# Hybrid SSD and GLA trunk: 21 units' y turned by transposing transfers, and the first block's gates reordered

## The chip, the cores and the metric

The kernel runs on one core of a Trainium2 chip. The metric is the device time of one execution in microseconds (us); lower is better. In the views of the profile PE is the matrix engine (PEld its weight loads), DVE the vector engine, ACT the scalar engine, POOL the general engine and SP the engine that issues most transfers. A name with q (ACTq, POOLq) is the engine's sequencer, where register work, waits and DMA issues are.

## What is computed

2048 tokens of width 1024, with 16 meta tokens in front, pass one layer of two parallel branches. Cut to what matters here:

```python
u = rmsnorm(hres, norm_w)
proj = jnp.einsum('bld,dn->bln', u, w_in)
z, xbc, dt_raw, q, k, v, g_gla, a_lr, merge_g = split_cols(proj, IN_WIDTHS)
xbc = jax.nn.silu(causal_depthwise_conv(xbc, conv_w, conv_b))
...
y = y.reshape(b, l, D_SSD) * jax.nn.silu(z)
y_ssd = rmsnorm(y.reshape(b, l, SSD_GROUPS, D_SSD // SSD_GROUPS),
                ssd_norm_w.reshape(SSD_GROUPS, -1)).reshape(b, l, D_SSD)
gate_logit = jnp.einsum('blr,rk->blk', a_lr, gla_gate_w2) + gla_gate_b
log_a = (jax.nn.log_sigmoid(gate_logit.astype(jnp.float32)) / GLA_GATE_TEMP)
...
o = rmsnorm(jnp.concatenate([o_m, o_r], axis=1), gla_norm_w)
y_gla = o.reshape(b, l, GLA_DV) * jax.nn.silu(g_gla)
branches = jnp.stack([y_ssd.astype(y_gla.dtype), y_gla], axis=2)
branch_proj = jnp.einsum('blnc,ncd->blnd', branches, w_branch)
gates = jax.nn.sigmoid(merge_g.reshape(b, l, N_BRANCH, D_MODEL))
merged = jnp.sum(gates * branch_proj, axis=2)
return hres + jnp.einsum('bld,de->ble', merged, w_out)
```

SSD is a scan over chunks of 128 tokens in 4 groups (256 channels each, a 128-wide state), GLA a gated linear attention with 4 heads of 256 value channels.

## The kernel before

**Tiling.** The tokens go in 4 blocks of 512 (`BLK`), the first with the 16 meta tokens in front (`m0` is 16 there and 0 elsewhere). In each block every SSD group and every GLA head is one unit: 4 + 4 units, 32 in all. After the blocks, from some 1500 us on, follow the products for the merge gates, the two branches and the output, which the change leaves alone. All large products are in single precision, made of three matmuls on high and low parts (`accum`, L205 to L209); so L207, L208 and L209 are the projections wherever they stand in a view.

**What sets the order.** PE's and SP's order is written by hand: `enter` (L950) yields one piece of a projection after another, and after each piece `step` advances every running generator by one yield. `begin` adds a generator. So a scan is a chain of short steps, each put on PE behind one piece of a projection. The order of DVE, ACT and POOL is left to a scheduler that sees the instructions' dependences; `tc.issue_after(x)` keeps what stands under it behind instruction x on its engine. Each engine works through its list in order, and each waits at an instruction whose operand isn't there.

**The units' ends.** `ssd_scan` (L588) works through 4 chunks of 128 tokens. `before(c)` turns the features (L634 on PE), makes xdt, xw and the skip part (L637 to L640, DVE), bt (L643, ACT) and the decay matrix dm (four L647 and one L649 on ACT, L650 on DVE). `after(c)` has the products L659, L660 and L662 on PE, the state's decay L664 (POOL) and its sum L665 (DVE), the output L667 to L672 (DVE) and its square sum L674 (ACT). When 4 chunks are done `rstd_of` gives the norm's factor (L251 on DVE, L252 on POOL), L689 scales the tile `yt` (tokens on partitions, 4 x 256 channels, from the pool "tok4" with 5 buffers) and the unit is turned to channels on partitions: 2 x 4 transposes of 128x128 on PE (L694) into two banks of PSUM (pool `pt`, 3 banks), two evictions with the channel weights on ACT (L696) into "gg", two stores to `y_left` that ACT issues (L697). `gla_scan` (L739) ends alike: scale L920 of `ot` (one buffer), transposes L925, then the product with the gate on DVE (L926) straight from PSUM, stores L929.

**The convolution** (`proj_conv`): ACT takes a projection out of PSUM twice (L565 raw, L566 scaled), DVE adds three shifted taps (L570), ACT's tanh (L573) and DVE's L574 end it.

**The GLA gates** (`gates`, L451): matmuls into PSUM, DVE's L473 and ACT's L474 read them, ACT's L476 and L477 make the logarithm for two heads at a time, then DVE subtracts (L480) and sums along the tokens (`tensor_tensor_scan`, L482). Their result `g_all` is read by `gla_scan` alone (from L751 on). In the first block `gates` begins at step 6 and `ssd_scan` of group 0 too. z's gates are L491 (ACT) and L492 (DVE).

**Others named below.** L334 to L336 prepare u of the next block (`fetch_u`; L335 is its store), L83 to L87 sum weights for the later products (`make_sums`, POOL and transfers), L171 and L172 split weights, `atp` holds GLA's attention split into two parts (L256, 2 buffers), L888 and L909 are PE's in GLA, L801 and L835 its levels and states. `behind()` keeps the decay matrices of the first block behind the last eviction of a projection.

Of the kernel before, what the change touches and what calls it, by code (L numbers as in the profile page):

```python
# [9 lines left out]
F32R = mybir.dt.float32r  # L10
BF16 = mybir.dt.bfloat16
U8 = mybir.dt.uint8
AF = mybir.ActivationFunctionType
ALU = mybir.AluOpType

P = 128
# [5 lines left out]
SG = 4  # L22
# [21 lines left out]
def trunk_kernel(ctx: ExitStack, tc: tile.TileContext, xm, xmt, w_feat, w_tok, w_v3, w_zm, w_br, w_o,  # L44
# [7 lines left out]
    def mk(pool, shape, dt, tag, **kw):  # L52
        cnt[0] += 1
        return pool.tile(shape, dt, tag=tag, name=f"{tag}_{cnt[0]}", **kw)
# [194 lines left out]
    def rstd_of(ssq, n, scale):  # L249
        r = mk(sm, [P, 4], F32, "rstd")  # L250
        nc.vector.tensor_scalar(r[:, :n], ssq, scale, EPS, op0=ALU.mult, op1=ALU.add)  # L251
        nc.gpsimd.tensor_tensor(r[:, :n], r[:, :n], mhalf[:, :n], op=ALU.pow)  # L252
        return r
# [197 lines left out]
    def gates(o):  # L451
        m0, tt, chunks, g_all = o.m0, o.tt, o.chunks, o.g_all
        ast = (mk(wk, [P, META + BLK], F32R, "act", bufs=NACT) if m0 else mk(wk, [P, BLK], F32R, "sq", bufs=NSQ))[:48, :tt]
        for a, n in ([(0, META), (m0, BLK)] if m0 else [(0, BLK)]):
            ps = bank(pt, "pt")
            for i, (ca, cn) in enumerate(chunks):
                if a <= ca < a + n:
                    nc.tensor.transpose(ps[:48, ca - a:ca - a + cn], o.alr[:cn, i], ident[:cn, :cn])
            nc.scalar.activation(ast[:, a:a + n], ps[:48, :n], AF.Copy)
            nc.vector.tensor_tensor(ast[:32, a:a + n], ps[:32, :n], ast[:32, a:a + n].bitcast(F32),  # L460
                                    op=ALU.subtract)
            nc.scalar.activation(ast[:16, a:a + n], ps[:16, :n], AF.Copy)
        yield
        for h2 in range(0, GH, 2):
            gmt = mk(wk, [P, 2, META + BLK], F32, "tok4", bufs=NT4)
            for h in (h2, h2 + 1):
                gm = gmt[:, h % 2, :tt]
                gb = gate_b[:, h:h + 1]
                for i, (a, n) in enumerate(o.segs_all):
                    ps = bank(*((pj, "pj") if m0 and i == 0 else (pt, "pt")))  # L470
                    nc.tensor.matmul(ps[:, :n], w2[:, h * P:(h + 1) * P], ast[:, a:a + n],
                                     start=True, stop=True)
                    nc.vector.tensor_scalar(gm[:, a:a + n], ps[:, :n], gb, 0.0, op0=ALU.add, op1=ALU.min)  # L473
                    nc.scalar.activation(g_all[:, h, a:a + n], ps[:, :n], AF.Abs, bias=gb)  # L474
            ga = g_all[:, h2:h2 + 2, :tt]
            nc.scalar.activation(ga, ga, AF.Exp, scale=-1.0)  # L476
            nc.scalar.activation(ga, ga, AF.Ln, bias=1.0)  # L477
            yield
            for h in (h2, h2 + 1):
                nc.vector.tensor_tensor(gmt[:, h % 2, :tt], gmt[:, h % 2, :tt], g_all[:, h, :tt], op=ALU.subtract)  # L480
                for a, n in chunks:
                    nc.vector.tensor_tensor_scan(g_all[:, h, a:a + n], ones[:, :n], gmt[:, h % 2, a:a + n], 0.0,  # L482
                                                 op0=ALU.mult, op1=ALU.add)
                yield


# [68 lines left out]
    def proj_conv(o, g):  # L555
        tt = o.tt
        feats = o.feats[g] = []
        for j in range(4):
            ti = g * 4 + j
            pss = proj_feat(f"s{ti}", w_feat[T_SSD + ti], o.segs_all, o.mov)  # L560
            cin = mk(spool, [P, 3 + META + BLK], F32, "cin")
            acc = mk(spool, [P, META + BLK], F32, "acc")[:, :tt]
            nc.scalar.activation(cin[:, 0:3], tails[:, ti, :], AF.Copy)
            for ps, (a, n) in zip(pss, o.segs_all):
                nc.scalar.activation(cin[:, 3 + a:3 + a + n], ps[:, :n], AF.Copy)  # L565
                evicted[:] = [nc.scalar.activation(acc[:, a:a + n], ps[:, :n], AF.Identity, scale=hcw[:, ti, 3:4],  # L566
                                                   bias=hcb[:, ti:ti + 1])]
            nc.gpsimd.tensor_copy(tails[:, ti, :], cin[:, tt:tt + 3])
            for k in range(3):
                nc.vector.scalar_tensor_tensor(acc, cin[:, k:k + tt], hcw[:, ti, k:k + 1], acc,  # L570
                                               op0=ALU.mult, op1=ALU.add)
            f = mk(wk, [P, META + BLK], F32, "act", bufs=NACT)
            nc.scalar.activation(f[:, :tt], acc, AF.Tanh)  # L573
            nc.vector.scalar_tensor_tensor(f[:, :tt], f[:, :tt], 1.0, acc, op0=ALU.add, op1=ALU.mult)  # L574
            feats.append(f)
            yield

    cbs, evicted = {}, []

    def behind():  # L580
        return tc.issue_after(evicted[-1].ins) if evicted else nullcontext()
# [2 lines left out]
    def fetch_cb(o, g, c):  # L584
        cbs[g, c] = cb = mk(spool, [P, 4, P], F32, "cb", bufs=3)
        nc.sync.dma_start(cb, o.cumd[4 * g:4 * g + 4, c * P:(c + 1) * P].unsqueeze(0).to_broadcast([P, 4, P]))

    def ssd_scan(o, g):  # L588
        m0, ci0 = o.m0, o.ci0
# [63 lines left out]
        def after(c):  # L653
            a = m0 + c * P
            ci = ci0 + c
            xdt, xw, bt, dm = held.pop(c)
            py = bank(pc, "pc")
            for h in range(4):
                nc.tensor.matmul(py[:, h * 64:(h + 1) * 64], dm[:, h], xdt[:, h], start=True, stop=True)  # L659
            nc.tensor.matmul(py[:, 256:512], cf[:, a:a + P], s_ssd[:, g], start=True, stop=True)  # L660
            pst = bank(pc, "pc")
            nc.tensor.matmul(pst[:, :256], bt, xw.rearrange("p a c -> p (a c)"), start=True, stop=True)  # L662
            sv = s_ssd[:, g].rearrange("p (h c) -> p h c", c=64)
            nc.gpsimd.tensor_tensor(sv, sv, hb(dec[:, ci, hs], P), op=ALU.mult)  # L664
            nc.vector.tensor_tensor(s_ssd[:, g], s_ssd[:, g], pst[:, :256], op=ALU.add)  # L665
            yo = mk(wk, [P, 4, 64], F32, "c1", bufs=NC1)
            nc.vector.tensor_tensor(yo, py[:, 256:512].rearrange("p (h c) -> p h c", c=64),  # L667
                                    hb(ecu[:, ci, hs], P), op=ALU.mult)
            yof = yo.rearrange("p a c -> p (a c)")
            nc.vector.tensor_tensor(yof, yof, py[:, 0:256], op=ALU.add)  # L670
            nc.vector.tensor_tensor(yof, yof, yt[:, c], op=ALU.add)
            nc.vector.tensor_tensor(yt[:, c], yof, o.zs[g][:, c], op=ALU.mult)  # L672
            jk = mk(wk, [P, 256], BF16, "junk", bufs=1)
            nc.scalar.activation(jk, yt[:, c], AF.Square, accum_out=ssq[:, c:c + 1])  # L674

        before(0)
        yield
# [2 lines left out]
            yield  # L680
        for c in range(1, NCH):
            before(c)
            after(c - 1)
            yield
        after(NCH - 1)
        yield
        r = rstd_of(ssq, 4, 1.0 / 1024)
        for c in range(NCH):
            nc.scalar.activation(yt[:, c], yt[:, c], AF.Identity, scale=r[:, c:c + 1])  # L689
        yield  # L690
        for j in range(2):
            ps = bank(pt, "pt")
# [46 lines left out]
    def gla_scan(o, h, last=False):  # L739
# [178 lines left out]
        r = rstd_of(ssq, 4, 1.0 / 256)  # L918
        for c in range(NCH):
            nc.scalar.activation(ot[:, c], ot[:, c], AF.Identity, scale=r[:, c:c + 1])  # L920
        yield
        for j in range(2):
            ps = bank(pt, "pt")
            for c in range(NCH):
                nc.tensor.transpose(ps[:, c * P:(c + 1) * P], ot[:, c, j * P:(j + 1) * P], ident)  # L925
            nc.vector.scalar_tensor_tensor(gs[j], ps, hgw[:, j:j + 1], gs[j], op0=ALU.mult, op1=ALU.mult)  # L926
# [7 lines left out]
    def begin(gen):  # L934
        begun.append(gen)
# [14 lines left out]
    def enter(pieces, o):  # L950
        b = o.b
        for n in range(6 * (SG + GH) + 1):
            i, r = divmod(n, 6)
            if r == 0:
                if 0 < i <= SG:
                    begin(ssd_scan(o, i - 1))
                elif i > SG and not (b == nblk - 1 and i - SG > LATE_G):
                    begin(gla_scan(o, i - SG - 1))
                if (b, i) in beside:
                    begin(beside_unit(beside[b, i]))  # L960
            if n == (8 if b else 6):
                begin(gates(o))
            if n == 6 * SG + (3 if b else 3):
                begin(fetch_u(b + 1) if b + 1 < nblk else first_b())
            if n < 6 * (SG + GH):
                yield next(pieces)
        assert next(pieces, pieces) is pieces
# [496 lines left out]
```

## Time and profile before

| | |
|---|---|
| median of 3 runs | 2273.96 us (2271.23 to 2276.47) |
| profiled execution | 2273.81 us, of which the span of the profile is 2271.3 |
| busiest engines | PE 2222.4, DVE 1565.7, ACT 1185.6, POOL 679.9 us |
| mean granted PE clock | 0.994 |

A row of the view by lines tells what a group of like instructions cost; a timeline row is start, duration, engine, line, instruction, and in brackets how long the engine had idled before it and what ended that. Matmuls overlap: PE's duration of one (0.39 us for 128x512) is longer than the step to the next (0.23 us).

### The profile page before, as it was taken

The page shows a single profiled execution, that of the slowest core. Times are in us where ns is not written, and L with a number is a line of the kernel's source. Part 1 is how long each engine was busy: PE and PEld are TensorE (multiplying, and loading weights), DVE is VectorE, ACT ScalarE, POOL GpSimd, SP SyncE. Part 2 cuts the span into 40 slices and gives each one's busy share as a digit, 9 for nine tenths or more (in the row PEclk, how much of TensorE's full clock was granted, in tenths as well). Part 3 has the DMA queues.
Part 4 walks back from the last instruction along what each step waited for, and adds up shares of the span by engine and source line. Part 5 has one row for each costly group of instructions (what it writes and reads, how often), then busy time and mean ns, then how long its engine had stood idle before and what let it go on. Part 6 is the DMA issues. An engine that isn't in the chain of part 4 may idle for free.

```text
span 2271.3 us, 34896 instructions
## 1 busy us (share of the span) xinstructions
PE 2222.4 (98%) x11789; PEld 1902.9 (84%) x11789; DVE 1565.7 (69%) x2935; ACT 1185.6 (52%) x2767; POOL 679.9 (30%) x681
## 2 busy tenths in 40 slices
PE   7999999999999999999999999999999999999998
PEld 6899989888888988888988888878888888888887
DVE  5777666677667676557677566674678955779876
ACT  4666655456544455544456454454554545554544
POOL 3334443122221112122122200056323264413341
PEclk9999999999999999999999999999999999999999
DMA  8666776667778667788676664366677866678763
GB/s 298 219 215 233 256 243 223 219 213 235 242 246 269 210 208 228 230 256 280 202 225 215 214 212 161 117 221 223 220 250 258 306 230 205 240 270 268 242 194 126
DMA packets 314210, 517.94 MB, mean 228 GB/s; under 512 B 28080, under 2 KB 162480, under 8 KB 314032
## 3 DMA queue, kind: packets, MB, share of 16 engines
q1 hardware_dynamic: 246864, 419.63, 57.4%
q10 hardware_dynamic: 67168, 96.10, 11.7%
q8 instruction: 92, 1.51, 0.3%
q14 instruction: 86, 0.70, 0.1%
HBM read 368.42 MB, written 147.19 MB: 227 GB/s over the span
## 4 chain that ended last, share of the span: by engine, by line
PE 87%; DVE 4%; ACT 3%; DMA 3%; issue 2%; POOL 1%; SPq 0%; POOLq 0%; ACTq 0%; DVEq 0%
PE pj L207 19%; PE pj L209 19%; PE pj L208 19%; PE pt L207 4%; PE pt L208 4%; PE pt L209 4%; PE pc L209 2%; PE pc L208 2%; PE pc L659 2%; PE pc L207 2%; PE pc L801 2%; PE pc L660 1%; PE pc L909 1%; PE pc L662 1%; PE pt L634 1%
## 5 line engine op out<-in xcount | busy, mean ns | idle before, releaser
L207 PE MATMUL pj<-ue,whl 128*128 128x264 f32 (+1 forms) x672 | 236.9, 353 | 8.4 <-ACT acc L566 4.1
L209 PE MATMUL pj<-ue,whl 128*128 128x264 f32 (+1 forms) x672 | 231.1, 344 | 0.8 <-DVE tkc L419 0.8
L208 PE MATMUL pj<-ue,whl 128*128 128x264 f32 (+1 forms) x672 | 230.2, 343 | 0.0
L207 PE MATMUL pj<-uo,whl 128*128 128x512 f32 x512 | 206.0, 402 | 0.0
L209 PE MATMUL pj<-uo,whl 128*128 128x512 f32 x512 | 200.1, 391 | 0.0
L208 PE MATMUL pj<-uo,whl 128*128 128x512 f32 x512 | 199.4, 389 | 0.0
L207 PE MATMUL pj<-b,a 128*128 128x512 f32 (+1 forms) x484 | 188.9, 391 | 1.5 <-ACT sn L1109 1.0
L209 PE MATMUL pj<-b,a 128*128 128x512 f32 (+1 forms) x484 | 188.8, 390 | 0.0
L208 PE MATMUL pj<-b,a 128*128 128x512 f32 (+1 forms) x484 | 188.0, 388 | 0.6 <-DVE b L1050 0.5
L570 DVE SCALAR_TENSOR_TENSOR acc<-cin,hcw,acc 128x512 f32<-128x512 f32 (+1 forms) x192 | 153.1, 798 | 50.2 <-ACT acc L566 49.2
L83 POOL TENSOR_TENSOR wr<-wr 128x256 f32<-128x256 f32 x80 | 66.8, 835 | 384.5 <-DMA wr<-y 162.6
L1065 POOL TENSOR_TENSOR as<-ar,ar 128x512 f32<-128x512 f32 x40 | 57.9, 1447 | 386.0 <-DMA ar<-in_w_br 103.2
L1075 DVE TENSOR_TENSOR a<-ar,a 128x512 fp32r<-128x512 f32 x160 | 129.3, 816 | 58.9 <-ACT a L1074 54.6
L1050 DVE TENSOR_TENSOR b<-br,b 128x512 fp32r<-128x512 f32 x140 | 124.7, 910 | 43.7 <-ACT b L1049 43.1
L207 PEld LDWEIGHTS pj<-ue,whl 128*128 128x128 f32 x672 | 127.7, 190 | 24.7 <-ACT acc L566 5.1
L209 PEld LDWEIGHTS pj<-ue,whl 128*128 128x128 f32 x672 | 127.8, 190 | 15.9 <-POOL whl L172 1.0
L208 PEld LDWEIGHTS pj<-ue,whl 128*128 128x128 f32 x672 | 127.8, 190 | 14.7
L1049 ACT ACTIVATE b<-br 128x512 fp32r<-128x512 f32 x140 | 86.5, 627 | 100.6 <-DMA br<-br_t 38.8
L172 POOL TENSOR_TENSOR whl<-wr,whl 128x512 fp32r<-128x512 f32 (+1 forms) x76 | 99.0, 1310 | 126.4 <-ACT whl L171 84.8
L1075 DVE TENSOR_TENSOR a<-as,a 128x512 fp32r<-128x512 f32 x120 | 105.5, 881 | 39.0 <-ACT a L1074 35.7
L1109 ACT ACTIVATE sn<-pj 128x512 f32<-128x512 f32 x118 | 69.8, 591 | 110.8 <-PE pj L209 69.5
L208 PE MATMUL pt<-b,a 128*128 128x512 f32 x320 | 125.3, 391 | 0.0
(329 smaller groups left out, 6470.7 us busy)
## 6 DMA issues: line engine op xcount, KB each, us to landing
whl<-k_s SPq DMA_DIRECT2D x96, 512.0 KB, 3.7
whl<-k_g SPq DMA_DIRECT2D x96, 512.0 KB, 4.2
whl<-k_v SPq DMA_DIRECT2D x36, 512.0 KB, 3.9
wr<-in_w_feat SPq DMA_DIRECT2D x64, 256.0 KB, 4.3
k_s<-whl SPq DMA_DIRECT2D x32, 512.0 KB, 3.7
cb<-cumd SPq DMA_DIRECT2D x64, 256.0 KB, 4.9
y<-gg ACTq DMA_DIRECT2D x64, 256.0 KB, 4.1
k_g<-whl SPq DMA_DIRECT2D x32, 512.0 KB, 3.7
```

The lines of the kernel that those rows point to most:

```text
L83: nc.gpsimd.tensor_tensor(o, x, y, op=ALU.subtract)
L172: nc.gpsimd.tensor_tensor(hl[:, 1], raw, hl[:, 0].bitcast(F32), op=ALU.subtract)
L207: nc.tensor.matmul(ps, sh, mh, start=first, stop=False, **kw)
L208: nc.tensor.matmul(ps, sh, ml, start=False, stop=False, **kw)
L209: nc.tensor.matmul(ps, sl, mh, start=False, stop=last, **kw)
L570: nc.vector.scalar_tensor_tensor(acc, cin[:, k:k + tt], hcw[:, ti, k:k + 1], acc, op0=ALU.mult, op1=ALU.add)
L659: nc.tensor.matmul(py[:, h * 64:(h + 1) * 64], dm[:, h], xdt[:, h], start=True, stop=True)
L1049: nc.scalar.activation(t[:, 0], raw, AF.Copy)
L1050: nc.vector.tensor_tensor(t[:, 1], raw, t[:, 0].bitcast(F32), op=ALU.subtract)
L1065: nc.gpsimd.tensor_tensor(s1, a21, a22, op=ALU.add)
L1075: latest[:] = [nc.vector.tensor_tensor(t[:, 1], src, t[:, 0].bitcast(F32), op=ALU.subtract)]
L1109: nc.scalar.activation(sn, self.ps[n, "a"], AF.Copy)
```

## The change

Three things.

1. In blocks 1 to 3 all 12 SSD units, and of GLA all heads of blocks 1 and 2 and the first of block 3 (9 units), are turned without PE. The new `turned` takes the tile as 16-bit words: ACT copies the low and the high halves into two tiles of 128x1024 words (from the pool of `atp`), ACT issues two transposing transfers (8 blocks of 128x128 words each) back into the source tile, and POOL interleaves the halves again with 4 copies into the two `atp` tiles. In SSD ACT then scales these in place (L721 in the changed kernel, for L696) and stores them from there; in GLA DVE's product reads them in place of PSUM.
2. In the first block `gates` begins ahead of `ssd_scan` of group 0; its subtraction and scans (L480, L482) stand behind the latest tap of the convolution (`convd`), one head after the other; the squares of SSD come a step later and behind the last eviction.
3. The first block begins to fetch u of the next block at step 24 in place of 27.

```diff
@@ gates
-                    nc.scalar.activation(g_all[:, h, a:a + n], ps[:, :n], AF.Abs, bias=gb)
+                    evicted[:] = [nc.scalar.activation(g_all[:, h, a:a + n], ps[:, :n], AF.Abs, bias=gb)]
...
             for h in (h2, h2 + 1):
-                nc.vector.tensor_tensor(gmt[:, h % 2, :tt], gmt[:, h % 2, :tt], g_all[:, h, :tt], op=ALU.subtract)
-                for a, n in chunks:
-                    nc.vector.tensor_tensor_scan(g_all[:, h, a:a + n], ones[:, :n], gmt[:, h % 2, a:a + n], 0.0,
-                                                 op0=ALU.mult, op1=ALU.add)
+                with tc.issue_after(convd[-1].ins) if m0 else nullcontext():
+                    nc.vector.tensor_tensor(gmt[:, h % 2, :tt], gmt[:, h % 2, :tt], g_all[:, h, :tt], op=ALU.subtract)
+                    for a, n in chunks:
+                        nc.vector.tensor_tensor_scan(g_all[:, h, a:a + n], ones[:, :n], gmt[:, h % 2, a:a + n], 0.0,
+                                                     op0=ALU.mult, op1=ALU.add)
                 yield
@@ proj_conv
             for k in range(3):
-                nc.vector.scalar_tensor_tensor(acc, cin[:, k:k + tt], hcw[:, ti, k:k + 1], acc,
-                                               op0=ALU.mult, op1=ALU.add)
+                convd[:] = [nc.vector.scalar_tensor_tensor(acc, cin[:, k:k + tt], hcw[:, ti, k:k + 1], acc,
+                                                           op0=ALU.mult, op1=ALU.add)]
@@ new
+    def turned(src):
+        flat = src.rearrange("p c f -> p (c f)").bitcast(U16)
+        words = flat.rearrange("p (n w) -> p n w", w=2)
+        tiles = [mk(wk, [P, BLK], F32, "atp", bufs=2) for _ in range(2)]
+        for w in range(2):
+            nc.scalar.activation(tiles[w].bitcast(U16), words[:, :, w], AF.Copy)
+        back = flat.rearrange("p (w k t) -> p w k t", w=2, t=P)
+        for w in range(2):
+            nc.scalar.dma_start_transpose(back[:, w], tiles[w].bitcast(U16))
+        for j in range(2):
+            dst = tiles[j].bitcast(U16).rearrange("p (c t w) -> p c t w", w=2, t=P)
+            for w in range(2):
+                nc.gpsimd.tensor_copy(dst[:, :, :, w], back[:, w].rearrange("p (c j) t -> p c j t", j=2)[:, :, j])
+        return tiles
@@ ssd_scan
-            jk = mk(wk, [P, 256], BF16, "junk", bufs=1)
-            nc.scalar.activation(jk, yt[:, c], AF.Square, accum_out=ssq[:, c:c + 1])
+            if not m0:
+                square(c)
+
+        def square(c):
+            with behind() if m0 else nullcontext():
+                jk = mk(wk, [P, 256], BF16, "junk", bufs=1)
+                nc.scalar.activation(jk, yt[:, c], AF.Square, accum_out=ssq[:, c:c + 1])
...
+            if m0 and c > 1:
+                square(c - 2)
             after(c - 1)
             yield
+        if m0:
+            square(NCH - 2)
         after(NCH - 1)
         yield
+        if m0:
+            square(NCH - 1)
         r = rstd_of(ssq, 4, 1.0 / 1024)
         for c in range(NCH):
             nc.scalar.activation(yt[:, c], yt[:, c], AF.Identity, scale=r[:, c:c + 1])
+        if not m0:
+            tiles = turned(yt)
+            for j in range(2):
+                nc.scalar.activation(tiles[j], tiles[j], AF.Identity, scale=hsw[:, 2 * g + j:2 * g + j + 1])
+            yield
+            for j in range(2):
+                nc.scalar.dma_start(y_left[0][o.b][2 * g + j], tiles[j])
+            return
         yield
@@ gla_scan
-        yield
-        for j in range(2):
+        by_dma = not m0 and not (o.b == nblk - 1 and h >= LATE_G - 1)
+        if by_dma:
+            for j, t in enumerate(turned(ot)):
+                nc.vector.scalar_tensor_tensor(gs[j], t, hgw[:, j:j + 1], gs[j], op0=ALU.mult, op1=ALU.mult)
+        else:
+            yield
+        for j in () if by_dma else range(2):
@@ enter
+                if i == 1 and b == 0:
+                    begin(gates(o))
                 if 0 < i <= SG:
                     begin(ssd_scan(o, i - 1))
...
-            if n == (8 if b else 6):
+            if b and n == 8:
                 begin(gates(o))
-            if n == 6 * SG + (3 if b else 3):
+            if n == 6 * SG + (3 if b else 0):
                 begin(fetch_u(b + 1) if b + 1 < nblk else first_b())
```

Two places of the engines' lists show it. The first is DVE in the first block, around the first two heads' gates: tok_135 is the gates' tile, c_ and s_ssd belong to SSD, acc_1215 to the convolution. Before:

```order
L650 TENSOR_TENSOR sq_1123<-sq_1123,sq_1106 128x512
L480 TENSOR_TENSOR tok_135_1130<-tok_135_1130,g_all_397 128x528 x2
L482 SCALAR_TENSOR_TENSOR g_all_397<-ones_r,tok_135_1130 128x16
L482 SCALAR_TENSOR_TENSOR g_all_397<-ones_r,tok_135_1130 128x128 x4
L482 SCALAR_TENSOR_TENSOR g_all_397<-ones_r,tok_135_1130 128x16
L482 SCALAR_TENSOR_TENSOR g_all_397<-ones_r,tok_135_1130 128x128 x4
L613 COPY s_ssd<-pc_1228 128x256
L570 SCALAR_TENSOR_TENSOR acc_1215<-cin_1214,hcw,acc_1215 128x528 x3
L574 SCALAR_TENSOR_TENSOR act_1225<-act_1225,acc_1215 128x528
```

In the changed kernel (tok_122 is the gates' tile; L667, L482, L484, L572 and L576 are L650, L480, L482, L570 and L574 of before):

```order
L667 TENSOR_TENSOR sq_1142<-sq_1142,sq_1125 128x512
L630 COPY s_ssd<-pc_1234 128x256
L572 SCALAR_TENSOR_TENSOR acc_1215<-cin_1214,hcw,acc_1215 128x528 x3
L482 TENSOR_TENSOR tok_122_1093<-tok_122_1093,g_all_397 128x528
L484 SCALAR_TENSOR_TENSOR g_all_397<-ones_r,tok_122_1093 128x16
L484 SCALAR_TENSOR_TENSOR g_all_397<-ones_r,tok_122_1093 128x128
L576 SCALAR_TENSOR_TENSOR act_1225<-act_1225,acc_1215 128x528
L484 SCALAR_TENSOR_TENSOR g_all_397<-ones_r,tok_122_1093 128x128 x3
```

The taps now stand ahead of the subtraction and the scans, and the second head's scans follow behind the next convolution's taps.

The second is ACT in block 1 at the end of the first SSD unit (tok_958 is its tile, sq_6436 the first decay matrix of the next unit). Before:

```order
L689 ACTIVATE tok_958_5934<-tok_958_5934,rstd_6323 128x256 x4
L474 ACTIVATE g_all_5230<-pt_6331,pv 128x512
...
L696 ACTIVATE gg_6398<-pt_6393,hsw 128x512
L696 ACTIVATE gg_6406<-pt_6401,hsw 128x512
L697 DMA y_1_0_104<-gg_6398 128x512
...
L647 ACTIVATE sq_6436<-cb_6341,tkc_5225 128x128 x4
...
L649 ACTIVATE sq_6436<-sq_6436 128x512
L643 ACTIVATE bt_6434<-pt_6425 128x128
```

In the changed kernel (L717, L475, L664, L666 and L660 are L689, L474, L647, L649 and L643 of before; sq_6434 is the decay matrix):

```order
L717 ACTIVATE tok_958_5934<-tok_958_5934,rstd_6323 128x256 x4
L595 ACTIVATE atp_6330<-tok_958_5934 128x1024
L595 ACTIVATE atp_6331<-tok_958_5934 128x1024
L475 ACTIVATE g_all_5230<-pt_6343,pv 128x512
...
L598 DMA_TRANSPOSE tok_958_5934<-atp_6330 128x8x128
L598 DMA_TRANSPOSE tok_958_5934<-atp_6331 128x8x128
...
L664 ACTIVATE sq_6434<-cb_6353,tkc_5225 128x128 x4
...
L721 ACTIVATE atp_6330<-atp_6330,hsw 128x512
L660 ACTIVATE bt_6432<-pt_6423 128x128
L666 ACTIVATE sq_6434<-sq_6434 128x512
```

Copies and issues now stand ahead of the decay matrices, and one scale of the turned tile ahead of the first bt and the first L666; the other scale and the stores come behind. On PE the eight L694 or L925 of each of the 21 units are gone, and nothing takes their place.

3 lines of the change are left out of this document (2 added, 1 removed).

## The prediction

> **What bounds the kernel now.** I read the page's busy shares first, then its chain that ended last, then the list of what PE waited for, and last the timelines around those waits.
>
> ```profile
> PE 2222.4 (98%) x11789; PEld 1902.9 (84%) x11789; DVE 1565.7 (69%) x2935; ACT 1185.6 (52%) x2767; POOL 679.9 (30%) x681
> PE 87%; DVE 4%; ACT 3%; DMA 3%; issue 2%; POOL 1%; SPq 0%; POOLq 0%; ACTq 0%; DVEq 0%
> ```
>
> PE is busy for 2222.4 of 2271.3 us and carries 87% of the chain. So time is won by taking instructions from PE or by ending one of its waits, and lost wherever PE's written order comes to an operand that is not there. Of the 49 us in which PE idles, these rows (engine and line, what it waited for, us, times, longest) touch the change:
>
> ```profile
> PE pt L634 <- ACT gg L696: 4.4, 3, 1.5
> PE pj L207 <- ACT acc L566: 4.1, 3, 2.6
> PE pj L207 <- ACT g_all L474: 2.7, 2, 1.6
> PE pc L659 <- DVE sq L650: 2.1, 2, 1.9
> ```
>
> A stall costs more than itself. The windows behind the 2.6 us and the 1.9 us stall, between them a stretch without one:
>
> ```profile
> core 0: us, PE busy (x) PEld busy (x) DVE busy (x) ACT busy (x) POOL busy (x), PEclk, DMA share, GB/s
> 101.20:104.60 3.40, 3.40 (x18) 3.40 (x17) 3.40 (x7) 2.07 (x6) 1.29 (x1) 0.50 0.06 20
> 104.60:110.00 5.40, 5.40 (x41) 4.87 (x40) 4.43 (x8) 3.67 (x13) 2.04 (x3) 1.00 0.96 267
> 128.50:131.90 3.40, 3.40 (x14) 3.03 (x14) 3.40 (x5) 1.25 (x4) 2.37 (x2) 0.50 1.02 330
> ```
>
> The granted clock is 0.50 for 3.40 us, then 1.00. Eighteen matmuls in 3.40 us would take 18 x 5.40/41 = 2.4 us at the later pace, so each such stall costs about 1.0 us on top.
>
> **Term 1, transposes leave PE: -18.3 us.**
>
> ```profile
> L694 PE MATMUL pt<-cst,tok x128: 270/272/328, 144.0 to 1350.8; 128*128 128x128 f32 x128
> L925 PE MATMUL pt<-cst,ot x128: 270/272/327, 348.3 to 1494.2; 128*128 128x128 f32 x128
> 703.77 1.04 PE L925 MATMUL pt<-cst,ot 128*128 128x128 f32 x8
> 704.65 1.06 PE L801 MATMUL pc<-sq 128*128 128x128 f32 x8
> ```
>
> The first two rows give min/median/max in ns of one transpose. They overlap, so the price is the step from start to start: eight from 703.77 to 704.65, 0.88 us, and 0.87 us in the other units of these blocks. 21 units x 0.87 = 18.3 us (168 transposes).
>
> **Term 2, L634's wait: -4.4 us, gross.** L634 waits for a pt bank that L696 has yet to empty. Without L694 and L696 in these blocks this wait has no cause left: 4.4 us by its row.
>
> **Term 3, the first block: -7 us.** DVE, ACT and PE around the longest stall:
>
> ```profile
> 87.14 2.41 DVE L480 TENSOR_TENSOR tok<-tok,g_all 128x528 f32<-128x528 f32 x2 [3.47 <-ACT g_all L477]
> 89.47 4.89 DVE L482 TENSOR_TENSOR_SCAN g_all<-ones_r,tok 128x16 f32<-128x16 f32 x10
> 94.60 2.36 DVE L570 SCALAR_TENSOR_TENSOR acc<-cin,hcw,acc 128x528 f32<-128x528 f32 x3
> 97.04 1.28 ACT L573 ACT_TABLE_LOAD   x1 [4.43 <-DVE acc L570]
> 99.87 0.39 PE L207 MATMUL pj<-ue,whl 128*128 128x264 f32 x1 [2.61 <-ACT acc L566]
> ```
>
> DVE does 7.2 us of gate subtraction and scans ahead of the convolution's taps L570. L573 on ACT waits 4.43 us for the taps, the next evictions L565/L566 stand behind it, and PE waits 2.61 us for the bank. The change puts the taps first and the scans behind them; what reads the scans is GLA, whose gl (L751) stands over two hundred rows later in ACT's order. So the 2.6 us go, and what is late next has no reader near. Starting the gates a little earlier and the squares a step later aims at the 2.7 us (L474) and the 1.9 us (L650). Sum 7.2 us, and the two half-clock stretches add 2.0: 9.2 us at most. At least: 2.6 + 1.0 = 3.6, if the other two waits only change their name, since all ACT work stays, in another order. The stall on L474 is likeliest to do that, for its evictions only move ahead of others: I take 7.
>
> **Term 4, ACT in the first turned SSD unit of each block: +11 us.** ACT gets two 128x1024 copies and two transfers' issue in place of two evictions. In blocks 1 to 3 the first unit falls where ACT is full (block 1; then two rows of lines, min/median/max ns):
>
> ```profile
> 509.75 1.71 ACT L689 ACTIVATE tok<-tok,rstd 128x256 f32<-128x256 f32 x4 [1.32 <-POOL rstd L252]
> 512.16 1.35 ACT L474 ACTIVATE g_all<-pt,pv 128x512 f32<-128x512 f32 x2 [0.70 <-DVE tok L473]
> 519.76 1.28 ACT L696 ACTIVATE gg<-pt,hsw 128x512 f32<-128x512 f32 x2
> 525.43 0.63 ACT L649 ACTIVATE sq<-sq 128x512 f32<-128x512 f32 x1
> L476 ACT ACTIVATE g_all<-g_all x8: 1058/1062/1088, 83.6 to 1215.8; 128x1024 f32<-128x1024 f32 x6, 128x1056 f32<-128x1056 f32 x2
> L697 ACTq DMA_DIRECT2D y<-gg x32: 321/326/362, 146.6 to 1352.0; - x32
> ```
>
> Who waits for L649:
>
> ```profile
> 526.09 0.72 DVE L650 TENSOR_TENSOR sq<-sq,sq 128x512 f32<-128x512 f32 x1 [0.86 <-ACT sq L649]
> 526.40 0.49 PE L634 MATMUL pt<-cst,act 128*128 128x128 f32 x3
> 526.87 1.10 PE L659 MATMUL pc<-c,sq 128*128 128x64 f32 x8
> ```
>
> L649 ends at 526.06, L650 follows at once, and PE starts L659 0.06 us behind it: no slack. Between L689's end at 511.46 and L649's end ACT idles 0.70 us. Added there: copies 2 x 1.06 (the 128x1024 row), issues 2 x 0.33 (the store's row; 42 in all), and one of the new scales L721, 0.64: 3.4 us. Removed: L696, 1.28. So L649 comes 2.1 - 0.7 = 1.4 us later. PE loses that, and the 0.87 + 1.5 us credited to this unit in terms 1 and 2 are waited away: 3.7 us, times 3 blocks, 11. Bounds: ends at 0 if the scheduler's interleaving leaves more holes than I see, and at 3 x (2.4 + 3.1) = 16.5 if the issue of a transposing transfer takes the 1.17 us that is the longest of an ACT issue (L335's) instead of 0.33. No transposing issue is in the trace; I take the common row.
>
> ```profile
> L335 ACTq DMA_DIRECT2D u<-act x8: 326/394/1168, 16.3 to 22.2; - x8
> 560.41 0.63 ACT L573 ACTIVATE act<-acc 128x512 f32<-128x512 f32 x1 [0.81 <-DVE acc L570]
> 562.19 0.60 ACT L565 ACTIVATE cin<-pj 128x512 f32<-128x512 f32 x1 [1.05 <-PE pj L209]
> ...
> 601.02 0.38 ACT L491 ACTIVATE tok<-pj 128x256 f32<-128x256 f32 x1 [0.48 <-PE pj L209]
> 601.89 0.38 ACT L256 ACTIVATE tok<-pj 128x256 fp32r<-128x256 f32 x1 [0.49 <-DVE tok L492]
> ```
>
> In the second unit ACT has 0.81 + 1.05 = 1.86 us of holes ahead of L565 for 2.78 us of copies and issues, and L696 (1.26) leaves before L649: about nothing. The third (from 599.65) is alike, with holes of 0.48 and three of 0.49 us. **Term 5**, these six: +2 us (0 to 6).
>
> **Term 6, the transfers, POOL and GLA: +1 us.** POOL gets 84 copies of 128x512 16-bit words. The rows nearest, then how long L697's 256 KB stores take to land, all DMA packets, and ACT at a GLA unit's end:
>
> ```profile
> L664 POOL TENSOR_TENSOR s_ssd<-s_ssd,dec x64: 607/613/1147, 100.3 to 1338.9; 128x256 f32<-128x256 f32 x64
> L1065 POOL TENSOR_TENSOR as<-ar,ar x40: 1281/1298/3076, 1490.9 to 2211.9; 128x512 f32<-128x512 f32 x40
> DMA to landing us min/median/max: 2.0/4.6/6.5
> DMA packets 314210, 517.94 MB, mean 228 GB/s; under 512 B 28080, under 2 KB 162480, under 8 KB 314032
> 698.71 1.71 ACT L920 ACTIVATE ot<-ot,rstd 128x256 f32<-128x256 f32 x4
> 715.43 0.40 ACT L256 ACTIVATE atp<-sq 128x256 fp32r<-128x256 f32 x1
> ```
>
> A copy costs 0.6 to 1.3 us; I take 0.8 (half the bytes of L1065's): 3.2 us a unit on an engine that is busy 30%. In GLA the scales end at 700.42, copies and issues at 703.2, and the next head's split into atp is at 715.43: less 3.2 us of POOL and 1.5 us for the two products that read the tiles (estimate: 2 x 0.79, a third of L570's 2.36), 7.5 us remain for the transfers, more than the longest 6.5. 42 transfers of 256 KB are 11 MB beside 518: no load on the queues if a transposing transfer moves like a store. Cover gone, each us beyond 7.5 holds ACT's split. Bounds: 0 and the first rival.
>
> Sum: -18.3 - 4.4 - 7 + 11 + 2 + 1 = -15.7 us. The profiled execution took 2273.8 us (span 2271.3 and 2.5 around it), 0.15 below the median of 2273.96: **2258 us**.
>
> **Rivals.**
>
> First, slower: the transposing pair lands late. In the first unit of a block one L721 stands in ACT's order ahead of the first bt (L643) and the first L649; behind it wait all dm of the group, then DVE's L650, then PE. The pair is issued by 511.46 + 2.12 + 1.35 + 0.38 (one eviction) + 0.66 = 516.0. From its landing to L659: two POOL copies 1.6, L721 0.64, bt 0.27, L649 0.63, L650 0.72, 3.9 us, due at 526.87. So 7.0 us are free; beyond them every us costs 3 us, one in each block. The sum turns to a loss at 7.0 + 15.7/3 = 12.2 us. For it: no row of the trace shows such a transfer and its bytes go 128 x 128 words at a time. Against it: 256 KB stores land in 6.5 us at most. At 17 us: 3 x 10 = +30, 2288. Beside this, the Trainium skill (VectorE: DVE Perf Modes, The three transpose paths) gives a 128x128 two-byte transpose 1309 ns by DMA; by that, as an estimate, eight blocks are 10.5 us, the pair one after the other 21, and the time by this rival's rule 2258 + 3 x 14 = 2300. The skill's DMA: Bandwidth & Descriptors, Latency and other measured facts, gives DMA_TRANSPOSE 261 GB/s instead, an estimated 1 us for 256 KB, which leaves the sum as it is. No run here shows either yet.
>
> Second, all of it is hidden: ACT finds holes, terms 4 to 6 are 0 and term 3 is whole: 2273.8 - 18.3 - 4.4 - 9.2 = 2242. For it, ACT is busy 52%; against it, the 0.06 us at L659.
>
> Third, the first block gives nothing: gates' evictions ahead of the first dm make L659 wait where L207 waited. 2258 + 7 = 2265. For it: every ACT piece there remains; against: 7.2 us of DVE leave the taps' way.
>
> Fourth, PE is freed and time stays: a POOL operation beside DVE is long (1.15 against 0.61), and so may DVE's be. 84 x 0.5 = 45 us of stretch; a third of it in chains that PE waits for eats the gain: 2273.
>
> **How the numbers follow.** Forecast 0.49, late transfers 0.16, all hidden 0.14, first block void 0.14, stretched chains 0.07. Range 2238 to 2284: from the second rival less 4 to between forecast and first rival. This kernel's runs spread so that less than 0.2% (4.5 us) can't be told from none. Faster 0.76 (forecast, second, third, less a little for their upper tails), same 0.07, slower 0.17.
>
> **What would show it.** Term 1: 168 fewer PE instructions, no gaps where they stood. Term 2 and 4: no L634 wait for gg, in its place a wait of 1 to 4 us of L659 (now L676) for DVE sq at the first chunk, once in blocks 1, 2 and 3. Term 3: no 2.6 us stall and no half clock near 100 us. Term 6: DMA_TRANSPOSE landing under 7 us. I am wrong if that wait is over 6 us or ACT stands at L721, if transfers take over 12 us, or if PE waits at GLA's heads.

## The result, and the profile after

The changed kernel takes 2329.5 us (median of 4 runs, 2322.05 to 2343.86) against 2273.3 for the kernel before (4 runs, 2271.23 to 2276.47). The ratio is 1.0253, 95% interval 1.0226 to 1.0281: slower by 56 us, where 2258 was forecast. The profiled execution is the longest of the four, 2343.86 us with a span of 2342.0, so its differences add up to 71 us and not to 56.

The page after, busy shares:

```profile
PE 2230.8 (95%) x11621; PEld 1902.1 (81%) x11621; DVE 1586.1 (68%) x2935; ACT 1220.1 (52%) x2809; POOL 749.6 (32%) x765
```

The list of PE's waits after (line, releaser: us in total, times, longest):

```profile
PE pc L676 <- DVE sq L667: 27.5, 7, 5.7
PE pt L924 <- DVE sq L915: 24.2, 7, 7.5
...
PE pj L208 <- issue: 6.1, 2, 3.5
```

PE has its 168 instructions fewer, yet is busy 8.4 us longer, and idle 111.2 us in place of 48.9. The sum closes: idle +62.3, busy +8.4, together 70.7, the span's difference. Busy time should have fallen by 18.3; the 26.7 us between are matmuls at the lower clock. The mean granted clock fell from 0.994 to 0.983, and (1 - 0.983) x 2342.0 less (1 - 0.994) x 2271.3 are 26 us. Most new stalls have a stretch at half clock with them, and it can be two or three times as long as the 3.40 us read from the profile before (the windows' PEclk column, at a stall in SSD and one in GLA):

```profile
core 0: us, PE busy (x) PEld busy (x) DVE busy (x) ACT busy (x) POOL busy (x), PEclk, DMA share, GB/s
527.60:531.00 3.40, 2.65 (x10) 2.55 (x11) 2.23 (x5) 3.40 (x10) 0.00 (x0) 0.50 0.60 208
531.00:534.40 3.40, 3.40 (x9) 2.66 (x8) 2.55 (x7) 0.34 (x3) 0.74 (x2) 0.50 0.11 43
534.40:537.80 3.40, 3.40 (x16) 2.75 (x15) 2.67 (x5) 1.24 (x4) 0.00 (x0) 1.00 0.23 42
732.40:735.80 3.40, 0.00 (x0) 0.00 (x0) 1.99 (x4) 0.60 (x1) 2.53 (x4) 0.50 0.59 156
735.80:739.20 3.40, 2.19 (x10) 2.10 (x11) 3.40 (x8) 2.25 (x6) 0.00 (x0) 0.50 1.00 402
739.20:742.60 3.40, 3.40 (x9) 2.64 (x8) 3.40 (x10) 1.65 (x5) 0.00 (x0) 0.50 0.73 254
742.60:746.00 3.40, 3.40 (x16) 2.80 (x15) 3.37 (x10) 0.73 (x2) 0.00 (x0) 1.00 0.45 130
```

Where the time went is read from the start of the same projection matmul (the n-th on L207, L208 after) in the two traces:

| n-th L207 | what lies there | before, us | after, us | later by |
|---|---|---|---|---|
| 744 | end of the first block | 416.0 | 413.5 | -2.5 |
| 1080 | block 1, SSD done | 698.2 | 706.6 | +8.4 |
| 1296 | block 1, GLA done | 847.8 | 877.7 | +29.9 |
| 1512 | block 2, SSD done | 1037.3 | 1077.6 | +40.3 |
| 1728 | block 2, GLA nearly done | 1183.3 | 1242.3 | +59.0 |
| 1992 | block 3, its turned GLA unit done | 1414.3 | 1485.0 | +70.7 |
| 3192 | near the end | 2252.5 | 2323.2 | +70.7 |

The loss lies in the blocks with turned units alone. The first sight of its cause is the transposing transfers' own rows (durations of the issue, ns min/median/max, then us to landing):

```profile
L598 ACTq DMA_TRANSPOSE tok<-atp x24: 1274/1435/3118, 510.6 to 1424.6; - x24
L598 ACTq DMA_TRANSPOSE ot<-atp x18: 1259/1322/2655, 712.1 to 1474.4; - x18
...
DMA to landing us min/median/max: 3.3/6.5/13.5
```

An issue takes ACT's sequencer 1.3 to 3.1 us (68 us over the 42), where a store's took 0.33. In the first turned unit the second issue blocks ACT (rows of ACT, DVE and PE in order of time):

```profile
512.04 2.66 ACTq L598 DMA_TRANSPOSE tok<-atp  x1
514.74 1.06 ACT L477 ACTIVATE g_all<-g_all 128x1024 f32<-128x1024 f32 x1 [2.87 <-issue]
...
521.44 4.62 DVE L484 TENSOR_TENSOR_SCAN g_all<-ones_r,tok 128x128 f32<-128x128 f32 x8
...
524.64 0.72 ACT L721 ACTIVATE atp<-atp,hsw 128x512 f32<-128x512 f32 x1
525.25 0.28 ACT L660 ACTIVATE bt<-pt 128x128 f32<-128x128 f32 x1
525.41 0.64 ACT L666 ACTIVATE sq<-sq 128x512 f32<-128x512 f32 x1
...
527.62 0.67 DVE L667 TENSOR_TENSOR sq<-sq,sq 128x512 f32<-128x512 f32 x1
528.35 1.97 PE L676 MATMUL pc<-c,sq 128*128 128x64 f32 x8 [5.67 <-DVE sq L667]
```

The issue also holds back the gates' logarithm (L477), on which DVE's scans (L484) wait. They end at 526.06, with five short instructions between them and the decay product: L666 has ended at 526.05, L667 begins at 527.62. So the last 1.6 of the 5.67 us lie in DVE's list and not in ACT's.

In GLA another engine stands. POOL and DVE after the first GLA unit, the timeline:

```profile
721.73 0.76 POOL L602 COPY atp<-ot 128x512 uint16<-128x512 uint16 x1 [12.48 <-DMA ot<-atp]
726.95 2.55 POOL L602 COPY atp<-ot 128x512 uint16<-128x512 uint16 x3 [4.46 <-DMA ot<-atp]
...
727.74 1.13 DVE L960 SCALAR_TENSOR_TENSOR gg<-atp,hgw,gg 128x512 f32<-128x512 f32 x1 [9.41 <-POOL atp L602]
...
737.00 0.69 PE L924 MATMUL pt<-cst,sq 128*128 128x128 f32 x2 [7.49 <-DVE sq L915]
```

The pair was issued from 712.1 on and its second half came at 726.95, 14.9 us later. The product L960 stands in DVE's list ahead of the next head's attention; DVE idles 9.41 us at it, the attention tile is late, and PE waits 7.49 us.

### The profile page after: what moved, and what is told of

Its sections match the earlier page's. It is cut to its first block, busy times and chain, and to the rows that moved or that the text cites. A ratio compares the mean times of both kernels' runs of the same rounds, so it can differ in the third digit from the quotient of the medians.

```text
span 2342.0 us, 34824 instructions
## 1 busy us (share of the span) xinstructions
PE 2230.8 (95%) x11621; PEld 1902.1 (81%) x11621; DVE 1586.1 (68%) x2935; ACT 1220.1 (52%) x2809; POOL 749.6 (32%) x765
## 3 DMA queue, kind: packets, MB, share of 16 engines
q10 hardware_dynamic: 111520, 107.11, 14.6%
## 5 line engine op out<-in xcount | busy, mean ns | idle before, releaser
L208 PE MATMUL pj<-ue,whl 128*128 128x264 f32 (+1 forms) x672 | 239.9, 357 | 10.0 <-issue 3.5
L210 PE MATMUL pj<-ue,whl 128*128 128x264 f32 (+1 forms) x672 | 233.6, 348 | 0.8 <-DVE tkc L420 0.8
L209 PE MATMUL pj<-ue,whl 128*128 128x264 f32 (+1 forms) x672 | 232.9, 347 | 0.0
L208 PE MATMUL pj<-uo,whl 128*128 128x512 f32 x512 | 210.4, 411 | 4.2 <-issue 2.6
L210 PE MATMUL pj<-uo,whl 128*128 128x512 f32 x512 | 203.3, 397 | 0.0
L209 PE MATMUL pj<-uo,whl 128*128 128x512 f32 x512 | 202.8, 396 | 0.0
L572 DVE SCALAR_TENSOR_TENSOR acc<-cin,hcw,acc 128x512 f32<-128x512 f32 (+1 forms) x192 | 158.8, 827 | 50.8 <-ACT acc L568 49.1
L208 PE MATMUL pj<-b,a 128*128 128x512 f32 (+1 forms) x484 | 189.1, 391 | 1.8 <-ACT sn L1152 1.3
L208 PEld LDWEIGHTS pj<-ue,whl 128*128 128x128 f32 x672 | 129.3, 192 | 26.7 <-issue 4.7
L1117 ACT ACTIVATE a<-ar 128x512 fp32r<-128x512 f32 x160 | 98.9, 624 | 52.4 <-PE pt L210 26.5
```

Source lines behind the costliest of these rows:

```text
L208: nc.tensor.matmul(ps, sh, mh, start=first, stop=False, **kw)
L209: nc.tensor.matmul(ps, sh, ml, start=False, stop=False, **kw)
L210: nc.tensor.matmul(ps, sl, mh, start=False, stop=last, **kw)
L572: convd[:] = [nc.vector.scalar_tensor_tensor(acc, cin[:, k:k + tt], hcw[:, ti, k:k + 1], acc, op0=ALU.mult, op1=ALU.add)]
L1117: nc.scalar.activation(t[:, 0], src, AF.Copy)
```

## The experiments

Times are medians; ratios are to the kernel before on the same chip, with 95% intervals. All keep the first block's part.

**The parts apart.** e1, e2 and e3 switch the transfers off with the two conditions; e4 replaces them by plain copies and so leaves the turn out.

```diff
@@ e1: both; e2: the first; e3: the second
-        if not m0:
-            tiles = turned(yt)
+        if False:
+            tiles = turned(yt)
...
-        by_dma = not m0 and not (o.b == nblk - 1 and h >= LATE_G - 1)
+        by_dma = False
@@ e4
-            nc.scalar.dma_start_transpose(back[:, w], tiles[w].bitcast(U16))
+            nc.scalar.dma_start(back[:, w].rearrange("p k t -> p (k t)"), tiles[w].bitcast(U16))
```

> The first block's part alone; all 32 units are turned on TensorE again. Late-transfer theory: the two traces stand 2.5 us apart at 420 us in favour of the change, so 2270 to 2272 us. Rival, the reordered first block carries part of the loss into later blocks: 2280 or more.

Measured 2274.6 us, ratio 0.9997 (0.9985 to 1.0009): neither. The first block's part is worth nothing that can be measured (at the 744th matmul e1 is 1.0 us ahead of the kernel before, where the changed kernel was 2.5 ahead).

> Only the 9 GLA units are turned by transfers (first block's part kept). Late-transfer theory: the profile's ledger puts about 50 of 71 us into GLA's stretches, so two thirds of the loss: 2305 to 2318 us, with PE's waits on the attention tile (L924 for DVE) there as in the change. Rival, the loss comes from SSD's ACT work: 2270 or below, nearly all GLA gain and no waits.

Measured 2314.7 us, 1.0173 (1.0149 to 1.0197): as the theory said, with 19.9 us of waits for the attention tile.

> Only the 12 SSD units are turned by transfers (first block's part kept). Late-transfer theory: about 24 of 71 us, so 2285 to 2297 us, waits of 3 to 6 us at L676 in the first and second unit of a block. Rival, SSD's ACT work is the whole loss: 2320 or more.

Measured 2302.4 us, 1.0123 (1.0104 to 1.0141): more than the ledger's 24 us, with 23.7 us of waits at L676 after the first block. The parts, +40 and +28, add up to 68, over the 56 of the whole.

> The changed kernel with both transfers of a unit as plain copies of the same 256 KB, same engine and place; the turn inside the 128x128 blocks is left out. Late-transfer theory: issue 0.33 us, landing near 4 us, no DVE wait over 3 us at L960, 2250 to 2275 us. Rival, the added copies on ACT and POOL are the cost: still over 2310.

Measured 2295.8 us, 1.0097 (1.0066 to 1.0129): between the two. The issue fell to 0.56 us and the landing to 4.4 us (medians), and 34 of 56 us went with it; 22 us stayed. Both theories held a part, so the next runs took waits away one at a time.

**The instruction in the way.** In e5, DVE's products go behind the next head's attention; in e6, ACT's copies go behind the next unit's first decay matrix; e7 does both; e8 turns only the unit that no SSD unit follows.

```diff
@@ e5
-            for j, t in enumerate(turned(ot)):
-                nc.vector.scalar_tensor_tensor(gs[j], t, hgw[:, j:j + 1], gs[j], op0=ALU.mult, op1=ALU.mult)
+            tiles = turned(ot, True)
+            yield
+            yield
+            yield
+            with tc.issue_after(attd[-1].ins):
+                for j, t in enumerate(tiles):
+                    nc.vector.scalar_tensor_tensor(gs[j], t, hgw[:, j:j + 1], gs[j], op0=ALU.mult, op1=ALU.mult)
@@ e6
-            tiles = turned(yt)
+            yield
+            yield
+            with tc.issue_after(dmd[-1].ins):
+                tiles = turned(yt)
@@ e8
-        if not m0:
+        if not m0 and g == 3:
```

`attd` and `dmd` hold the latest attention tile's last DVE instruction and the latest L666.

> As e2 (GLA alone turned by transfers), but the two DVE products that read the turned tiles stand behind the next head's attention on DVE, and the tiles come from the ring of act instead of that of the attention tiles. Theory of the instruction in the way (DVE stands at the product while the pair lands): PE's waits for the attention tile (about 20 us in e2) go, and with them the half-clock stretches: 2274 less 7.8 us of PE plus a few: 2264 to 2276 us. Rival, the pair itself (ACT issue, POOL copies, queues) is the cost: still 2300 or more.

Measured 2302.3 us, 1.0119 (1.0100 to 1.0138): between. DVE no longer stands at the product, and PE's waits for the attention tile fell to 4.9 us, but 28 of 40 us stayed. Two new waits of 4 us stand at the decay product of the next block's first SSD unit (PE L679 for DVE L670, 8.0 us). The largest stall is now at the issue (timeline of ACT, then PE):

```profile
702.66 3.65 ACTq L601 DMA_TRANSPOSE ot<-act  x1
706.35 4.05 ACTq L601 DMA_TRANSPOSE ot<-act  x1
710.45 0.38 ACT L257 ACTIVATE tok<-pj 128x256 fp32r<-128x256 f32 x1 [6.75 <-issue]
...
711.39 0.77 PE L208 MATMUL pj<-uo,whl 128*128 128x512 f32 x1 [7.04 <-issue]
```

Two issues hold ACT for 7.7 us while PSUM banks that PE needs wait for ACT's eviction L257. The windows (last columns: clock, DMA share, GB/s) say when:

```profile
702.00:704.00 2.00, 2.00 (x14) 1.77 (x13) 0.70 (x2) 1.70 (x4) 0.00 (x0) 1.00 1.13 376
...
708.00:710.00 2.00, 0.00 (x0) 0.00 (x0) 0.00 (x0) 0.00 (x0) 0.00 (x0) 0.50 1.55 108
```

The transfers are issued while the DMA engines are full (share 1.13, 376 GB/s), and later the engines are as busy at a low rate (1.55, 108 GB/s). A theory of the landing alone does not give this wait.

> As e3 (SSD alone turned by transfers), but each unit's copies and transfers stand on ACT behind the next unit's first decay matrix. Theory of ACT's full stretch (copies and issues ahead of the first decay matrix make PE wait at L676): waits of the first and second unit go, 2274 less 12 x 0.87 and some of the 4.4 us at the turned features: 2260 to 2270 us. Rival, ACT stands at the scale L721 for the landing, wherever it is put: other waits (evictions L567) take their place, 2290 or more.

Measured 2284.9 us, 1.0043 (1.0024 to 1.0062): between, 18 of 28 us won. Waits at L676 after the first block fell from 23.7 to 5.8 us, while ACT stood 11 times, 19.3 us in all, at the scale for POOL's copies. (The profiled execution took 2277.5 us, 7 us less than the median, so its waits are those of a good run.)

> Both of these together, with the first block's part: if both theories hold the sum, 2250 to 2268 us; if either falls, over 2285.

Measured 2300.1 us, 1.0098 (1.0073 to 1.0122): the whole isn't won back.

> Only the last SSD group of blocks 1 to 3 (3 units) is turned by transfers, which no further SSD unit follows; the rest on TensorE, first block's part kept. Theory of ACT's full stretch: no wait at L676, 2274 less 2.6: 2270 to 2273 us. Rival, each turned unit costs alike (28 us over 12 units in e3, 2.3 each): 2281.

Measured 2278.1 us, 1.0016 (1.0006 to 1.0026): no wait at L676, yet 3.4 us slower. Three units with no full stretch behind them still lose 1.1 us each.

**The issuing engine.** e10 hands the transfers to SP, a step after the copies; e12 is its twin on ACT; e11 does it for SSD, e9 for both.

```diff
@@ e12 to e10
-            nc.scalar.dma_start_transpose(back[:, w], tiles[w].bitcast(U16))
+            nc.sync.dma_start_transpose(back[:, w], tiles[w].bitcast(U16))
@@ turned in e9 to e12, as a generator (first: dmd's in SSD; hold: 1 in SSD but for its last group)
+        with tc.issue_after(first.ins) if first else nullcontext():
+            for w in range(2):
+                nc.scalar.activation(tiles[w].bitcast(U16), words[:, :, w], AF.Copy)
+        yield
...
+        for _ in range(hold):
+            yield
+        with tc.issue_after(decd[-1].ins) if hold else nullcontext():
+            for j in range(2):
...
```

`decd` holds the latest state decay on POOL.

> GLA alone turned by transfers, products behind the next head's attention as in e5, staged in the head's own dead tiles (kd and qg); the two transposing transfers are issued by SP a step after ACT's copies, not by ACT. Theory of the issue (a transposing transfer holds its issuing engine's sequencer 1.3 to 4 us, and on ACT that keeps PSUM banks full): the 7 us waits of PE after L840 go, 2266 to 2276 us. Rival, the transfers disturb the other queues wherever they are issued: 2290 or more.

Measured 2333.6 us, 1.0250 (1.0230 to 1.0269): in the rival's range.

> The twin of e10 in which ACT issues the two transfers at the same step. Theory of the issue: slower than e10 by the waits behind the issue, 10 to 28 us more. Rival: within 4 us of e10.

Measured 2301.5 us, 1.0110 (1.0096 to 1.0125): 32 us faster than its twin, against both expectations. On SP the transfers land early (min/median/max 3.1/3.2/4.4 us), but SP's list holds the weights' loads. PE's waits in e10:

```profile
PE pj L208 <- DMA whl<-k_g: 22.6, 5, 6.1
PE pj L208 <- DMA whl<-k_s: 13.6, 2, 7.0
...
PE pj L208 <- DMA whl<-k_z: 9.4, 2, 5.0
```

45.6 us of waits for weights that the trace of e12 hasn't. The timeline of ACT, SP and PE at the first of the nine units shows why:

```profile
696.24 0.38 SPq L330 DMA_DIRECT2D acc<-in_xmt  x1
705.57 2.01 ACT L599 ACTIVATE act<-ot 128x1024 uint16<-128x1024 uint16 x2 [0.97 <-POOL wr L84]
707.60 2.75 SPq L603 DMA_TRANSPOSE ot<-act  x2
710.44 1.02 SPq L168 DMA_DIRECT2D whl<-k_g  x2
714.99 0.76 PE L208 MATMUL pj<-uo,whl 128*128 128x512 f32 x1 [6.11 <-DMA whl<-k_g]
```

SP stands at the pair until ACT's copies have ended at 707.58; the pair itself takes 2.75 us of SP. The load behind it is issued at 710.44, in e12 at 699.68, so of 10.8 us 8 are the wait for the copies. SP issued nothing for 9.9 to 12.9 us ahead of each of the nine pairs. So e10 doesn't show that SP issues a transposing transfer at a higher price than ACT: the larger part is again an instruction in the way, now in SP's list. And the short landings came with no loads of weights just issued. An order in which SP doesn't wait for the copies was not tried.

> SSD alone turned by transfers, copies behind the next unit's first decay matrix, transfers issued by SP, POOL's copies behind a later state decay, scales behind a later decay matrix. Theory of the issue and of the instruction in the way: 2285 of e6 falls to 2260 to 2272 us. Rival, other queues disturbed (weights late behind SP's issue): 2280 or more.

Measured 2320.2 us, 1.0205 (1.0187 to 1.0222), with 28.8 us of PE's waits for the weights k_g: the rival. Here too SP stands at L603 for ACT, up to 14.2 us at a time.

> e10 and e11 together. If the theories hold: 2250 to 2265 us, below the kernel before. Rival: the sum of e10's and e11's losses.

Measured 2379.3 us, 1.0452 (1.0433 to 1.0471): e10's and e11's losses (58 and 44 us) together.

**Transfers without copies, copies without transfers.** e13 turns on TensorE and adds 42 transposing transfers that nothing reads; e14 has the change without its transfers, POOL reading the source tile, and leaves the turn out.

```diff
@@ e13, called for yt and ot of the 21 units
+    def extra(src):
+        flat = src.rearrange("p c f -> p (c f)").bitcast(U16)
+        for w in range(2):
+            t = mk(wk, [P, BLK], F32, "atp", bufs=2)
+            nc.scalar.dma_start_transpose(t.bitcast(U16).rearrange("p (k t) -> p k t", t=P), flat[:, w * 2 * BLK:(w + 1) * 2 * BLK])
@@ e14
-        for w in range(2):
-            nc.scalar.dma_start_transpose(back[:, w], tiles[w].bitcast(U16))
...
-                nc.gpsimd.tensor_copy(dst[:, :, :, w], back[:, w].rearrange("p (c j) t -> p c j t", j=2)[:, :, j])
+                nc.gpsimd.tensor_copy(dst[:, :, :, w], words.rearrange("p (c j t) w -> p c j t w", j=2, t=P)[:, :, j, :, w])
```

> All 32 units are turned on TensorE (as e1), and 21 of them also issue two transposing transfers of the changed kernel's size from the same tile into the two free attention tiles, which nothing reads: the transfers' issue on ACT, their queue and their hold on tiles, without ACT's and POOL's copies and without a reader that waits. Theory of the issue and the queue: 15 to 35 us over e1, with PE waits put down to issue. Rival, only the wait for the landing costs: within 5 us of e1 (2274.5).

Measured 2307.7 us, 1.0145 (1.0125 to 1.0164): 33 us over e1, although nothing reads what they bring. PE's waits and ACT's:

```profile
PE pt L657 <- ACT gg L740: 15.5, 4, 5.4
...
ACT g_all L475 <- issue: 11.0, 3, 4.3
ACT sq L257 <- issue: 8.7, 2, 5.1
ACT act L575 <- issue: 7.9, 3, 3.5
```

ACT is held at the issue, evicts late, and PE waits for the bank. Two things keep this from being the price of the change's transfers. The eviction that PE waits for, L740, belongs to the turn on TensorE, which the change has not in these units. And twice ACT waits for a tile that a transfer still holds (8.3 us). By the starts of the projection matmuls e13 loses 10, 13 and 13 us against e1 in the SSD stretches of the three blocks, and in GLA's 3.5 us in all.

> The changed kernel without its 42 transfers: ACT's copies, POOL's interleaving (from the source tile) and the later steps stay, the turn is left out. Theory of the added engine work in SSD (ACT's copies ahead of the first decay matrix): 2265 to 2285 us, waits at L676 in the first unit of a block stay at 2 to 4 us, GLA's waits gone. Rival, all of the loss lies in the transfers: 2274 less 18 to 23, 2251 to 2256 us.

Measured 2283.8 us, 1.0034 (1.0022 to 1.0046): the theory of the added work. PE's waits after 400 us:

```profile
PE pc L674 <- DVE sq L665: 10.3, 6, 3.2
PE pc L677 <- DVE c L685: 4.5, 2, 2.5
```

By the starts of the same projection matmuls, the 0.88 us that a unit saves is a step at unit after unit (11.3, 10.4, 9.5 and 8.6 us late against the kernel before at n = 1848, 1872, 1920 and 1992). It is given back around the first turned unit of each block: +3.8 us from n = 864 to 912, +7.4 from 1296 to 1344, +7.0 from 1728 to 1800.

## Why the prediction was wrong, by its own steps

**What bounds the kernel** was right: PE's 98%, and every us lost is a wait of PE for an operand or a bank, with the half clock behind it.

**Term 1** (-18.3) held. 168 transposes are gone and in e14 each unit gains 0.88 us.

**Term 2** (-4.4, gross): the wait at L634 is gone where SSD is turned, and as term 4 foresaw L676 waits in its place.

**Term 3** (-7) failed. The 2.6 us stall on the taps went as argued, but the gate subtraction set behind the taps is now ahead of the decay product. DVE and PE in e1:

```profile
120.02 1.31 DVE L482 TENSOR_TENSOR tok<-tok,g_all 128x528 f32<-128x528 f32 x2
121.25 0.41 DVE L688 TENSOR_TENSOR c<-c,tok 128x256 f32<-128x256 f32 x1
121.58 1.75 DVE L667 TENSOR_TENSOR sq<-sq,sq 128x512 f32<-128x512 f32 x1
...
123.39 1.91 PE L676 MATMUL pc<-c,sq 128*128 128x64 f32 x8 [3.10 <-DVE sq L667]
```

PE waits 3.10 us there (1.91 before), the half clock is granted behind it for 6.8 us (3.4 before), and e1 is level. The third rival was the right one for this part, its place another: "what is late next has no reader near" looked at the scans' reader and not at what is queued behind them.

**Term 4** (+11) had the right place, and the stall itself came out where no transfer is issued: without the issue its rows give 2.12 + 0.64 - 1.28 - 0.70 + 0.87 + 1.5 = 3.15 us, and e14 waits 3.23, 3.12 and 2.98 us in the three first units. Two steps failed. The first: the term has nothing for the half clock behind its own stall, though the prediction had priced that at 1.0 us a stall. In e14 it lasts 6.8 us behind the first of them, and between n = 876 and 888 that kernel loses 6.4 us, twice the stall. The second is "I take the common row" for the issue: 0.33 us was taken, 1.17 was its upper bound, and the issue measured 1.3 to 3.1 us in the change and up to 4.2 us in e5. With transfers the three stalls are 5.67, 4.70 and 4.73 us. The bound came from plain transfers; a transposing one is another thing.

**Term 5** (+2, the second and third unit) failed with it. L676 waits 3.55 us at 577 us in the changed kernel; e3 has seven such waits after the first block.

**Term 6** (+1) is the largest miss, in two steps. First, "no load on the queues if a transposing transfer moves like a store": it does not. The packets of the ACT queue went from 67168 to 111520, 1056 for each 256 KB transfer, and e13 is 33 us slower than e1 with 42 transfers that nothing reads. Second, the window of 7.5 us in GLA was counted to ACT's split of the next head, with nothing between; DVE's own product stands earlier, in front of the attention that PE waits for (9.41 us of DVE at L960, 7.49 us of PE at L924).

**The first rival** (the pair lands late, a loss from 12.2 us on) named the right instrument. Pairs took 7.6 to 14.9 us in the first six units of block 1, from the first issue to POOL's first copy behind both landings. Its price, 3 us for each us beyond 7.0 at L721, missed the issue and DVE. The 1309 ns that the Trainium skill gives for one block (VectorE: DVE Perf Modes, The three transpose paths) don't add up eightfold here, as the prediction's estimate had them: on SP all eight landed 3.2 us (median) after the issue, 0.4 us a block. The 261 GB/s of the Trainium skill (DMA: Bandwidth & Descriptors, Latency and other measured facts) is nearer, but not reached: the share of ACT's queue (q10) grew by 15.2% of 2312.7 less 11.6% of 2273.6 us from e1 to e13, 88 us for 42 transfers or 2.1 us each on all 16 engines, 125 GB/s as an estimate.

**The other rivals.** The second (all hidden) is refuted by e14: the added engine work alone loses 8 us. The fourth (stretched chains) is there in part: DVE is busy 1586.1 us in the change and 1584.0 in e14, against 1565.7 before and 1564.6 in e13, which has no POOL copies. Whether PE ever waits for these 20 us is not shown. (Its 45 us are 84 x 0.54; with the 0.5 that it names they are 42.) Of the signs of being wrong three came: ACT stood at L721 six times (17.7 us), single transfers took up to 13.5 us, and PE waited at GLA's heads. The fourth, a wait at L676 over 6 us, stayed just out with 5.67.

**The sum as measured**, in medians: e13 loses 33 us against e1, e14 8 against the kernel before, together 41, and the change 56. These are not parts of one sum, as the branches show:

| | SSD, 12 units | GLA, 9 units |
|---|---|---|
| turned by transfers (e3, e2) | +28 | +40 |
| transfers that nothing reads (e13 to e1, profiled executions, by the starts of the matmuls) | +36 | +3.5 |

In SSD the transfers of e13 cost more than the whole change there, since they delay evictions that the change doesn't have. In GLA they cost 0.4 us a unit, less than the 0.87 that they would save: there the loss needs copies, transfers and a reader together. Moving the reader (L960) out of the way won 12 of the 40 us (e5), moving the copies and issues in SSD 18 of the 28 (e6). How the rest splits between the issue, the landing and POOL's copies was not tried and stays open.

No version among the fourteen beats the kernel before by more than its noise.

## What to carry to other kernels

A transfer's price has three parts: the issuing engine's sequencer, the queue, and the landing. Each is to be taken from a row of that kind of transfer, since a plain store's row bounds none of them for a transposing one. Work that is taken from a full engine and given to half-idle ones is paid where those run their lists in order: before moving it, find the instruction in each list that will stand and wait, and what stands behind it. Last, price the half clock of every stall that a change makes: of the 14 stalls of PE of 2 us or more between 400 and 1500 us here, 12 had a stretch of 3.4 to 10.2 us at a granted clock of 0.50 with them, two (2.50 and 2.01 us) had none.

## What the runs showed of the hardware

The issue of a 256 KB transposing transfer held its sequencer for 1.24 us at least on SP (e10) and 1.25 on ACT (e6), and up to 4.2 us on ACT (e5), where plain copies between the same tiles took 0.47 to 0.67 (e4). The landing was 6.5 us from ACT in the change and 3.2 from SP in e10 (medians), there with no loads of weights issued for 9.9 us or more. A stall of 1.91 us was enough for 3.4 us at a granted clock of 0.50 in the kernel before; stalls of 3.23 us (e14) and 5.67 us (the change) had 6.8 us of it.
